# mLSTM branch: a block's exponentials issued one step ahead of its scores, in halves of shared E buffers

## The chip, the cores and the metric

The kernel runs on one core of a Trainium2 chip. A core has five engines that each work through a queue of their own: TensorE (PE in the profile, with its weight loads shown apart as PEld), VectorE (DVE), ScalarE (ACT), GpSimd (POOL) and SyncE (SP), which here only issues DMAs. They run side by side and wait for one another through semaphores. The metric is the device time of one execution in microseconds (us); the time of a kernel is the median over several executions.

## The reference

One layer of a hybrid encoder block, 512 tokens by 1024 channels in float32. An RMS norm is followed by one wide projection; three token mixers take their parts of it: a bidirectional mLSTM, a neighbourhood attention on an 8 by 64 grid, and a cross-attention into 256 memory tokens. Their outputs are gated, merged and projected, and a convolutional GLU feed-forward layer follows.

The change lies in the mLSTM. Per head and direction, with log gates `log_i`, `log_f` and their running sum `a`, it computes

```
D = a[..., :, None] - a[..., None, :] + log_i[..., None, :]
D = jnp.where(causal, D, -jnp.inf)
qk = jnp.einsum('bhcjd,bhcsd->bhcjs', q, k)
P = jnp.exp(D - m_j[..., None]) * qk
num = jnp.einsum('bhcjs,bhcsd->bhcjd', P, v) + inter_w[..., None] * (state of earlier chunks times q)
h = num / jnp.maximum(jnp.abs(den), jnp.exp(-m_j))[..., None]
```

where `den` is the same sum with the normaliser in place of `v`. There are four heads of width 128 and two directions whose results are added.

## The kernel before, in words

**The work as a whole.** TensorE does nearly everything that takes long. A float32 product is made of three matmuls on operands that were split into a high and a low part (`mm3`, lines 212 to 215). Weights come from HBM in 141 blocks of 512 KB and some smaller ones (line 159, issued by SyncE, three buffers); ScalarE copies the high part (L195) and VectorE subtracts to get the low part (L196). Both have to keep ahead of TensorE, and everything else that the two engines do is queued between these splits.

**The mLSTM inside it.** The generator `ml_all` gives the mLSTM in small steps, which the main program runs between projections through `step`. The kernel uses chunks of 128 tokens, so a head has four blocks, J = 0 to 3. The gates are prepared once (`ml_prep`, `spread`). Then, for each head:

- `load_head` loads two 128x512 tiles `R`, one for each direction, with the row part of the log weights spread over all partitions (L660). Four such buffers exist, so head h+2 uses those of head h, once their last reader is done. The cross-attention, which comes later, takes its split operands `X` from the same four buffers (tag "R", `prep` in `xa_all`, splits at L219 and L220).
- `mask` adds the causal mask to `R` (L666), `edges` makes the weights of the edge blocks (L673, L675), `keys` splits the keys and weighs the values (L681 to L704), and `states` computes the states at the block ends (L722 to L736, splits at L219 and L220).
- `weights_J` makes a block's weights: the score matmul on TensorE (L748), two exponentials on ScalarE, one for each direction (L752, 128x128 each), and on VectorE the product of the two (L753).
- `values_J` multiplies them with the values on TensorE (L761, and L763 for the edge state), takes the absolute denominator (L774 or L776), floors and inverts it (L778, L779), and scales and sums the outputs (L780 to L785, squares at L787).
- `normalise` takes the norm's power on GpSimd (L793), the scaling by it follows on ScalarE (L798), and `emit_y` transposes and splits the branch's result (L806, L808).

`weights_J` of block J+1 stands ahead of `values_J` of block J. The tile `E` (128 x 4 x 128, two buffers) is taken anew for each block, which uses the first half of it; the second half stays empty here, since the neighbourhood attention, which shares the tag, needs the full width later.

**What sets the order.** A scheduler orders the instructions of each engine when the kernel is built, from the program's order, the dependencies and the buffers that are free by its own account of time. On the chip each engine then works in that fixed order. `issue_after(st["act"])` only keeps the exponentials behind the last one of `spread`.

Of the kernel before, what the change touches and what calls it, by code (L numbers as in the profile page):

```python
# [11 lines left out]
F32 = mybir.dt.float32  # L12
F32R = mybir.dt.float32r
AF = mybir.ActivationFunctionType
# [3 lines left out]
P = 128  # L18
S = 512
# [91 lines left out]
def hybrid_block(ctx, tc, xg, xT, memT, wflat, vecs, gbias, nabias, outa, outb, outc):  # L111
    nc = tc.nc
    V, A, G, PE, SY = nc.vector, nc.scalar, nc.gpsimd, nc.tensor, nc.sync
# [5 lines left out]
    tp = ctx.enter_context(tc.tile_pool(name="tp", bufs=2))  # L119
# [6 lines left out]
    def nm(s):  # L126
        uid[0] += 1
        return f"{s}_{uid[0]}"
# [7 lines left out]
    def tiny(n):  # L136
        return tp.tile([P, 32], F32, tag="tiny", name=nm("y"), bufs=12)[:, :n]
# [4 lines left out]
    def atps():  # L142
        return atp.tile([P, 512], F32, tag="at", name=nm("at"))
# [4 lines left out]
    st = {"raw": 0, "split": 0}  # L148
# [262 lines left out]
    for k in range(KT):  # L411
# [12 lines left out]
        for f in range(4):  # L424
            fs = slice(f * P, (f + 1) * P)
            if k == 0 and f == 0:
                hs = (slice(0, S // 2), slice(S // 2, S))
# [118 lines left out]
    ml = {}  # L546
# [105 lines left out]
    def ml_all():  # L652
# [3 lines left out]
        def load_R(h):  # L656
            R = []
            for d in range(2):
                t = tp.tile([P, S], F32, tag="R", name=nm("R"), bufs=4)
                SY.dma_start(t, rd[d, h].partition_broadcast(P))  # L660
                R.append(t)
            return R
# [5 lines left out]
        def edges(h, R, ee):  # L668

            mh, eq = ml["mh"], ee[:, :2 * P].rearrange("p (i c) -> p i c", i=2)  # L670
            for i in range(2):
                J, d = 3 * i, 1 - i
                A.activation(eq[:, i, :], R[d][:, J * P:(J + 1) * P], AF.Exp, bias=mh[:, J - 1 + 2 * d, d, h:h + 1])  # L673
            qe = qT[:, h * S:(h + 1) * S].rearrange("p (j c) -> p j c", j=4)[:, 0:4:3, :]
            V.tensor_tensor(eq, eq, qe, op=ALU.mult)  # L675
# [35 lines left out]
        def states(h, k, w, C, q, eq, R):  # L711

            flush()
            dec = ml["dec"]
            (ke, kh, kl), (ew, wh, wl) = k, w
            pc = [atps() for _ in range(2)]
            po = (0, 130, 0, 131)
            at = lambda J, d: pc[J // 2][:, po[J] + 129 * d:po[J] + 129 * d + 129]
            for J in range(NT):
                if J in (0, 3):  # L720
                    e = J // 3
                    PE.matmul(at(J, e), ke[:, e * P:(e + 1) * P], ew[e], start=True, stop=True)  # L722
                else:
                    o, js = po[J], slice((J - 1) * P, J * P)
                    mm3(pc[J // 2][:, o:o + 258], kh[:, js], kl[:, js], wh[J - 1], wl[J - 1], True, True)
            tj = [tp.tile([P, 2 * M], F32, tag="nab", name=nm("C")) for _ in range(2)]
            pair = lambda j, d: tj[j][:, 129 * d:129 * d + 129]
            one = [t[:, 258:387] for t in tj]
            C.extend([[pair(0, 0), pair(1, 0), one[0]], [one[1], pair(0, 1), pair(1, 1)]])
            for d in range(2):  # L730
                last = None
                for i in range(3) if d == 0 else range(2, -1, -1):
                    if last is None:
                        A.activation(C[d][i], at(i + d, d), AF.Copy)
                    else:
                        V.scalar_tensor_tensor(C[d][i], C[d][last], dec[:, d, i + d - 1, h:h + 1], at(i + d, d),  # L736
                                               op0=ALU.mult, op1=ALU.add)
                    last = i
            for j in range(2):
                split_act(wh[j], wl[j], tj[j][:, :258])  # L740

        def weights_J(h, J, R):

            bi = ml["bi"]
            js, hs = slice(J * P, (J + 1) * P), slice(h * S + J * P, h * S + (J + 1) * P)
            ps = atps()
            kq = ps[:, 384:512]
            PE.matmul(kq, kT[:, hs], qT[:, hs], start=True, stop=True)  # L748
            E = tp.tile([P, 4, P], F32, tag="E", name=nm("E"))[:, 0:2, :]
            for d in range(2):  # L750
                with tc.issue_after(st["act"]):
                    A.activation(E[:, d, :], R[d][:, js], AF.Exp, bias=bi[:, d, J, h:h + 1])  # L752
            V.tensor_tensor(E, E, kq.unsqueeze(1).to_broadcast([P, 2, P]), op=ALU.mult)  # L753
            return E, ps

        def values_J(h, J, E, ps, k, w, C, q, eq, R, H, ss):
            js = slice(J * P, (J + 1) * P)
            pv = ps[:, :260].rearrange("p (d c) -> p d c", d=2)
            for d in range(2):
                inter = (J, d) in ((0, 1), (NT - 1, 0))  # L760
                PE.matmul(pv[:, d, 0:129], E[:, d, :], va[:, J, h, 0:129], start=True, stop=not inter)  # L761
                if inter:
                    PE.matmul(pv[:, d, 0:129], eq[:, J // (NT - 1), :], C[d][J - 1 + d], start=False, stop=True)  # L763
            den = tiny(2)
            both = J in (1, 2)
            if both:
                pi = mmps()[:, :258]
                qs = slice((J - 1) * P, J * P)
                mm3(pi, q[0][:, qs], q[1][:, qs], w[1][J - 1], w[2][J - 1], True, True)
                pi = pi.rearrange("p (d c) -> p d c", d=2)  # L770
                sc = ml["sc"][:, J, :, h]
                V.tensor_tensor(den, pi[:, :, 128], sc, op=ALU.mult)
                V.tensor_tensor(den, den, pv[:, :, 128], op=ALU.add)
                A.activation(den, den, AF.Abs)  # L774
            else:
                A.activation(den, pv[:, :, 128], AF.Abs)  # L776
            emv = em[:, J, :].rearrange("p (a b) -> p a b", b=4)
            V.tensor_tensor(den, den, emv[:, 0:9:8, h], op=ALU.max)  # L778
            V.reciprocal(den, den)  # L779
            A.activation(H[:, js], pv[:, 0, 0:128], AF.Copy, scale=den[:, 0:1])  # L780
            V.scalar_tensor_tensor(H[:, js], pv[:, 1, 0:128], den[:, 1:2], H[:, js], op0=ALU.mult, op1=ALU.add)
            if both:
                V.tensor_tensor(den, den, sc, op=ALU.mult)
                for d in range(2):
                    V.scalar_tensor_tensor(H[:, js], pi[:, d, 0:128], den[:, d:d + 1], H[:, js], op0=ALU.mult, op1=ALU.add)  # L785
            sq = scr(128)
            A.activation(sq, H[:, js], AF.Square, accum_out=ss[:, J:J + 1])  # L787

        def normalise(H, ss):
            v = tiny(4)  # L790
            V.tensor_scalar(v, ss, 1.0 / 128.0, EPS, op0=ALU.mult, op1=ALU.add)
            rs = tiny(4)
            G.tensor_tensor(rs, v, nhalf[:, :4], op=ALU.pow)  # L793

            def scale():
                for J in range(NT):
                    js = slice(J * P, (J + 1) * P)
                    A.activation(H[:, js], H[:, js], AF.Copy, scale=rs[:, J:J + 1])  # L798

            late.append(scale)  # L800
# [13 lines left out]
        prev = None  # L814
        E = None
        def load_head(h):
            return load_R(h), tp.tile([P, S], F32, tag="H", name=nm("ee"), bufs=4)
# [4 lines left out]
        for h in range(4):  # L822
            if prev:
                values_J(h - 1, 3, *E, *own, *prev)
                normalise(*prev)
            states(h, *st_h)
            own = st_h
            R = own[-1]
            ee, nxt = nxt[1], load_head(h + 1) if h < 3 else None
            yield  # L830
            H = tp.tile([P, S], F32, tag="H", name=nm("H"), bufs=4)
            ss = tiny(4)
            if h == 0:
                edges(0, R, ee)
                for d in range(2):
                    mask(R, d)
            E = weights_J(h, 0, R)
            yield
            for J in range(1, NT):
                E2 = weights_J(h, J, R)  # L840
                if J == 3 and h < 3:
                    st_h = keys(h + 1, *nxt)
                values_J(h, J - 1, *E, *own, H, ss)
                E = E2
                if J == 1 and prev:
                    emit_y(h - 1, prev[0])
                if h < 3:
                    late.append((lambda g=h + 1, n=nxt: edges(g, *n), lambda n=nxt: mask(n[0], 0),
                                 lambda n=nxt: mask(n[0], 1))[J - 1])
                yield  # L850
            prev = (H, ss)
# [223 lines left out]
    yml = []  # L1075
    so = []
    gens.append(ml_all())

    xq = unit()
# [427 lines left out]
```

## Time and profile before

| | us |
|---|---|
| time before, median of 3 runs (875.71 to 876.38) | 876.06 |
| the profiled execution's own time | 875.70 |
| its span, first to last instruction | 873.9 |
| first and last exponential of the mLSTM (L752) | 126.1 and 221.7 |
| first and last value matmul (L761) | 135.2 and 231.4 |

The difference of 1.8 between the profiled time and its span lies around the span. The profile gives a page (busy time of each engine, 40 slices of the span, DMA queues, the chain that ended last, the costliest groups) and answers on the trace: who waited for whom, busy time by stage, and a timeline in which a row holds the start in us, the length in us, the engine, the line of the code, the operation, out<-in by tile names, the number of instructions that the row holds, and in brackets the idle time of the engine before it with what ended it. Lengths of neighbouring instructions overlap by some 0.1 us on ScalarE and VectorE, so the cost of an instruction in a full queue is the distance from its start to the next one's start.

### The profile page before, as it was taken

The numbers are of one execution on the slowest core, as the hardware profiler recorded it, in microseconds if no ns is written. First come the engines' busy times: TensorE is split into PE (matmuls) and PEld (weight loads), VectorE is DVE, ScalarE is ACT, GpSimd is POOL, SyncE is SP. The second block draws the span as 40 slices with busy tenths as digits, with TensorE's granted clock in tenths as the row PEclk, the third lists the DMA queues.
The fourth block names the chain that finished last, engine by engine and source line by source line (L and its number), as shares of the span: only waits on it lengthen the run. The fifth ranks groups of instructions, "written<-read, shape, count | busy, mean of one in ns | idle before, by whom it ended". The sixth has DMA issues, their size and how long they took to land.

```text
span 873.9 us, 12229 instructions
## 1 busy us (share of the span) xinstructions
PE 868.1 (99%) x4303; PEld 736.2 (84%) x4303; DVE 594.2 (68%) x1240; ACT 472.7 (54%) x996; POOL 125.2 (14%) x201
## 2 busy tenths in 40 slices
PE   9999999999999999999999999999999999999997
PEld 7898888888888888888888888888888888888887
DVE  7794789886677758897676658776633466666534
ACT  7563567765456658888544455444422344444532
POOL 0101100000163370600000002111100011111010
PEclk9999999999999999999999999999999999999999
DMA  8224633422242353533223432222233222222412
GB/s 281 99 77 148 210 123 125 166 82 90 95 132 81 111 161 108 158 120 122 98 97 109 145 108 97 97 97 96 76 100 104 107 97 97 97 97 90 142 34 97
DMA packets 39421, 99.81 MB, mean 114 GB/s; under 512 B 5688, under 2 KB 13880, under 8 KB 39360
## 3 DMA queue, kind: packets, MB, share of 16 engines
q1 hardware_dynamic: 31568, 92.32, 30.7%
q0 software_dynamic: 7360, 6.32, 3.2%
q8 instruction: 34, 0.56, 0.3%
q10 hardware_dynamic: 432, 0.39, 0.1%
q14 instruction: 27, 0.22, 0.1%
HBM read 94.80 MB, written 4.21 MB: 113 GB/s over the span
## 4 chain that ended last, share of the span: by engine, by line
PE 94%; DVE 3%; ACT 1%; issue 1%; DMA 1%; POOL 0%; POOLq 0%; SPq 0%
PE mm L214 28%; PE mm L213 28%; PE mm L215 28%; PE at L214 2%; PE at L215 2%; PE at L213 2%; PE at L938 1%; PE at L919 1%; PE at L761 1%; DMA R<-rd 1%; DVE wl L196 0%; PE at L900 0%; PE at L901 0%; PE at L1026 0%; PE at L243 0%
## 5 line engine op out<-in xcount | busy, mean ns | idle before, releaser
L213 PE MATMUL mm<-u,wh 128*128 128x512 f32 (+1 forms) x1072 | 414.6, 387 | 0.0
L215 PE MATMUL mm<-u,wl 128*128 128x512 f32 (+1 forms) x1072 | 411.9, 384 | 0.0
L214 PE MATMUL mm<-u,wh 128*128 128x512 f32 (+1 forms) x1072 | 411.6, 384 | 0.0
L195 ACT ACTIVATE wh<-wr 128x512 fp32r<-128x512 f32 (+2 forms) x298 | 183.9, 621 | 213.5 <-PE mm L214 168.2
L196 DVE TENSOR_TENSOR wl<-wr,wh 128x512 fp32r<-128x512 f32 (+3 forms) x300 | 203.9, 681 | 89.5 <-ACT wh L195 86.7
L215 PEld LDWEIGHTS mm<-u,wl 128*128 128x128 f32 x1072 | 201.4, 188 | 40.0
L213 PEld LDWEIGHTS mm<-u,wh 128*128 128x128 f32 x1072 | 201.6, 188 | 38.6 <-ACT wh L195 0.2
L214 PEld LDWEIGHTS mm<-u,wh 128*128 128x128 f32 x1072 | 201.6, 188 | 38.4
L1371 POOL TENSOR_TENSOR s<-s,rb 128x512 f32<-128x512 f32 x22 | 38.1, 1732 | 403.4 <-DVE s L1370 239.0
L542 POOL DMA_DIRECT2D u<-nav_d x128 | 62.5, 533 | 66.2 <-PE at L938 23.0
L219 ACT ACTIVATE u<-s 128x512 fp32r<-128x512 f32 x26 | 16.4, 632 | 57.7 <-DVE s L1374 56.2
L1374 DVE TENSOR_TENSOR s<-mm,s 128x512 f32<-128x512 f32 x22 | 15.2, 690 | 23.8 <-POOL s L1371 23.8
L462 ACT ACTIVATE s<-pad,vec 128x512 f32<-128x512 f32 x30 | 24.4, 813 | 9.4 <-DVE pad L460 9.4
L220 DVE SCALAR_TENSOR_TENSOR u<-s,u 128x512 fp32r<-128x512 f32 x26 | 19.1, 733 | 14.1 <-ACT u L219 14.0
L463 DVE SCALAR_TENSOR_TENSOR s<-pad,vec,s 128x512 f32<-128x512 f32 x30 | 22.5, 750 | 5.4 <-ACT s L462 5.2
L1370 DVE SCALAR_TENSOR_TENSOR s<-s,s 128x512 f32<-128x512 f32 x22 | 15.2, 692 | 13.4 <-ACT s L1369 13.3
L464 DVE SCALAR_TENSOR_TENSOR s<-pad,vec,s 128x512 f32<-128x512 f32 x30 | 22.5, 750 | 0.9
L1369 ACT ACTIVATE s<-s 128x512 f32<-128x512 f32 x22 | 13.9, 632 | 14.9 <-DVE s L1368 14.9
L460 DVE TENSOR_TENSOR pad<-mm,rb 128x512 f32<-128x512 f32 x22 | 15.1, 690 | 6.4 <-PE mm L215 6.2
L213 PE MATMUL mm<-wh,u 128*128 128x512 f32 x48 | 18.8, 392 | 0.0
L215 PE MATMUL mm<-wh,u 128*128 128x512 f32 x48 | 18.7, 390 | 0.0
L214 PE MATMUL mm<-wl,u 128*128 128x512 f32 x48 | 18.7, 390 | 0.0
(341 smaller groups left out, 1043.6 us busy)
## 6 DMA issues: line engine op xcount, KB each, us to landing
wr<-wflat SPq DMA_DIRECT2D x141, 512.0 KB, 3.2
nab<-nabias SPq DMA_DIRECT2D x16, 256.0 KB, 2.6
u<-nav_d POOLq DMA_DIRECT2D x128, 32.0 KB, 2.6
s<-xT SPq DMA_DIRECT2D x15, 256.0 KB, 3.7
wr<-wflat SPq DMA_DIRECT2D x14, 192.0 KB, 2.3
nav_d<-nv POOLq DMA_DIRECT2D x8, 256.0 KB, 3.0
R<-rd SPq DMA_DIRECT2D x8, 256.0 KB, 4.6
wr<-wflat SPq DMA_DIRECT2D x2, 544.0 KB, 3.1
```

Source lines behind the costliest of these rows:

```text
L195: A.activation(h[:, u:v], src, AF.Copy)
L196: V.tensor_tensor(l[:, u:v], src, h[:, u:v].bitcast(F32), op=ALU.subtract)
L213: PE.matmul(ps, lh, rh, start=start, stop=False)
L214: PE.matmul(ps, lh, rl, start=False, stop=False)
L215: st["mm"] = PE.matmul(ps, ll, rh, start=False, stop=stop).ins
L219: A.activation(h, src, AF.Copy, scale=scale)
L220: V.scalar_tensor_tensor(l, src, scale, h.bitcast(F32), op0=ALU.mult, op1=ALU.subtract)
L462: A.activation(t1, pad[:, 0:512], AF.Identity, scale=vcol(w, i), bias=vcol(b, i))
L463: V.scalar_tensor_tensor(t1, pad[:, 1:513], vcol(w, n + i), t1, op0=ALU.mult, op1=ALU.add)
L464: V.scalar_tensor_tensor(t1, pad[:, 2:514], vcol(w, 2 * n + i), t1, op0=ALU.mult, op1=ALU.add)
L542: G.dma_start(vw[r * 32:(r + 1) * 32, i * 256:(i + 1) * 256], nav_v[hf, r, CW[b]:CW[b] + 32, hp * 256:(hp + 1) * 256])
L1371: G.tensor_tensor(c, c, rb2, op=ALU.mult)
```

## The change

The two exponentials leave `weights_J` and become a function of their own, `expos(h, J, R)`. It takes a new `E` buffer for J = 0 and 2 only, and gives block J the half `J % 2` of it, so two buffers hold four blocks. It is called one step earlier than before: for J = 0 behind `states` of the head (for head 0 behind its masks), and for J = 1 to 3 behind `weights_J` of the block before.

```
--- before.py
+++ after.py
-        def weights_J(h, J, R):
+        Eb = []
+
+        def expos(h, J, R):
+
+            if J % 2 == 0:
+                Eb[:] = [tp.tile([P, 4, P], F32, tag="E", name=nm("E"))]
+            E = Eb[0][:, J % 2 * 2:J % 2 * 2 + 2, :]
+            for d in range(2):
+                with tc.issue_after(st["act"]):
+                    A.activation(E[:, d, :], R[d][:, J * P:(J + 1) * P], AF.Exp, bias=ml["bi"][:, d, J, h:h + 1])
+            return E
+
+        def weights_J(h, J, E):
...
-            E = tp.tile([P, 4, P], F32, tag="E", name=nm("E"))[:, 0:2, :]
-            for d in range(2):
-                with tc.issue_after(st["act"]):
-                    A.activation(E[:, d, :], R[d][:, js], AF.Exp, bias=bi[:, d, J, h:h + 1])
             V.tensor_tensor(E, E, kq.unsqueeze(1).to_broadcast([P, 2, P]), op=ALU.mult)
             return E, ps
...
             ee, nxt = nxt[1], load_head(h + 1) if h < 3 else None
+            if h > 0:
+                En = expos(h, 0, R)
             yield
...
                 for d in range(2):
                     mask(R, d)
-            E = weights_J(h, 0, R)
+                En = expos(0, 0, R)
+            E = weights_J(h, 0, En)
+            En = expos(h, 1, R)
             yield
             for J in range(1, NT):
-                E2 = weights_J(h, J, R)
+                E2 = weights_J(h, J, En)
+                if J < 3:
+                    En = expos(h, J + 1, R)
                 if J == 3 and h < 3:
                     st_h = keys(h + 1, *nxt)
                 values_J(h, J - 1, *E, *own, H, ss)
```

No instruction is added or removed. What moves is seen in the built programs. On TensorE and GpSimd the order stays, but for one matmul: in head 2 the third matmul of a group (L215) now stands ahead of the value matmuls of block 0 (L761) and not behind them. On SyncE the two `R` loads of head 2 stand two to three weight blocks earlier, those of head 3 three. On ScalarE and VectorE the order changes in each head. ScalarE's queue in head 0, from its first exponential on (J and d are block and direction; line numbers are those of before):

```
before                                  after
L752 J0 d0                              L752 J0 d0
L1089 tanh, L311                        L1089 tanh, L311
L752 J1 d0                              L752 J1 d0, J2 d0, J3 d0
L693, L703 x2, L734, L703               L693, L734, L703
L219, L195, L219                        L219, L195, L219
L752 J0 d1, J1 d1                       L752 J0 d1, J1 d1, J2 d1, J3 d1
L703                                    L703 x2
L195                                    L195
table load, L337 (Ln)                   table load, L337 (Ln)
table load, L1089 tanh, L338            table load, L1089 tanh, L338
L195 x2                                 L195, L703, L195
L752 J2 d0, L1089, L776, L752 J2 d1     L776, L1089
L780                                    L780
```

And the two queues ahead of head 2's first product of scores and exponentials:

```
ScalarE before                          ScalarE after
L219 state, L798 x4, L219 state         L798 x4, L219 state, L219 state
L195                                    L195, L703, L219 X (128x512)
L195                                    L195

VectorE before                          VectorE after
L220 state, L736, L220 state            L736, L220 state, L220 state
L196                                    L196, L704, L220 X (128x512)
L1121, L753 J0, L753 J1                 L1121, L753 J0, L753 J1
```

Ahead of that stretch, and ahead of the same one in heads 1 and 3, ScalarE has the exponentials of blocks 2 and 3 of the head where it had those of block 1. Ahead of head 3's first product the two queues also get the two 128x256 splits of `X`.

More of the change, by code (lines that the diff above doesn't have):

```diff
@@ L740, in states @@
                 split_act(wh[j], wl[j], tj[j][:, :258])
-        def weights_J(h, J, R):
-            bi = ml["bi"]
-            js, hs = slice(J * P, (J + 1) * P), slice(h * S + J * P, h * S + (J + 1) * P)
+        Eb = []
[8 more added lines that the diff above has]
+        def weights_J(h, J, E):
+            hs = slice(h * S + J * P, h * S + (J + 1) * P)
             ps = atps()
```

## The prediction

> **What bounds the kernel now.** I read the page first, then the waits of TensorE and of its weight loads, then the busy time by stage, and last the timelines of ScalarE, VectorE and TensorE around the few places where TensorE waits inside the mLSTM. The page:
>
> ```profile
> PE 868.1 (99%) x4303; PEld 736.2 (84%) x4303; DVE 594.2 (68%) x1240; ACT 472.7 (54%) x996; POOL 125.2 (14%) x201
> ...
> PEclk9999999999999999999999999999999999999999
> ```
>
> TensorE is never without work for long and holds its full clock. What it waited for because of the weights `E`, from the list of waits (engine and line, what released it, us in total, times, longest):
>
> ```profile
> PE at L761 <- DVE E L753: 0.4, 1, 0.4
> ...
> PEld at L761 <- DVE E L753: 1.1, 3, 0.6
> ...
> ACT E L752 <- PE at L761: 3.7, 5, 1.5
> ```
>
> The first two rows are all the waits of TensorE that the exponentials can have a part in: at most 1.5 us, and the two overlap, since a weight load and its matmul wait for the same product. So the change has at most 0.17% to win. What it can lose is not bounded in this way, because ScalarE and VectorE work in a fixed order and the first one is asked to do things earlier than they are needed. The stage with the largest wait, from the busy time by stage (length, then busy us of PE, PEld, DVE, ACT, POOL, then granted clock):
>
> ```profile
> 135.00:145.00 10.00, 9.59 (x60) 8.40 (x59) 9.59 (x29) 7.22 (x22) 0.83 (x1) 1.00 0.33 119
> ```
>
> VectorE is as full there as TensorE, and TensorE's missing 0.41 is the wait of the first list.
>
> **Head 0: a pair of table loads moves back.** ScalarE in head 0 is busy without a gap from the first exponential to the tanh of the output gate:
>
> ```profile
> 129.99 0.68 ACT L752 ACTIVATE E<-R,bi 128x128 f32<-128x128 f32 x2
> 130.58 0.39 ACT L703 ACTIVATE u<-u,wt 128x129 fp32r<-128x129 f32 x1
> 130.87 0.62 ACT L195 ACTIVATE wh<-wr 128x512 fp32r<-128x512 f32 x1
> 131.51 1.28 ACT L337 ACT_TABLE_LOAD   x1
> 132.80 0.38 ACT L337 ACTIVATE s<-at 128x256 f32<-128x256 f32 x1
> 133.20 1.28 ACT L1089 ACT_TABLE_LOAD   x1
> 134.50 0.63 ACT L1089 ACTIVATE s<-s 128x512 f32<-128x512 f32 x1
> ```
>
> Start to start, two exponentials cost 0.59 and one L703 0.29. In the new order the four exponentials of blocks 2 and 3 stand ahead of these table loads (4 x 0.295 = 1.18), and one L703 has gone behind them (0.29). So the tanh starts 0.89 later, at 135.39. VectorE's queue behind it:
>
> ```profile
> 133.46 0.61 DVE L704 SCALAR_TENSOR_TENSOR u<-u,wt,u 128x129 fp32r<-128x129 f32 x2
> 135.16 0.43 DVE L1098 TENSOR_SCALAR u<-s 128x512 f32<-128x512 f32 x1 [1.09 <-ACT s L1089]
> ...
> 140.06 0.35 DVE L781 SCALAR_TENSOR_TENSOR H<-at,y,H 128x128 f32<-128x128 f32 x1 [0.25 <-ACT H L780]
> ...
> 143.10 0.41 DVE L753 TENSOR_TENSOR E<-E,at 128x256 f32<-128x256 f32 x1
> ```
>
> VectorE idles for that tanh already, and then works nearly without a gap up to the product at 143.10, so the product moves with the tanh. Of the stretch between them the new order takes out the idle 0.25 ahead of L781 (the floor and the reciprocal, L778 and L779, stand further ahead) and puts in one L704 (0.27, half of the distance in its row, moved back from 133.46). With some hundredths of rounding the product of block 2 starts 0.83 later, at 143.93. Its exponentials, which are early now, were not what it waited for. TensorE's rows there:
>
> ```profile
> 142.55 0.60 PE L681 MATMUL at<-ident,u 128*128 128x128 f32 x4
> 143.56 0.71 PE L761 MATMUL at<-u,E 128*128 128x129 f32 x4 [0.41 <-DVE E L753]
> ```
>
> The value matmul starts 0.46 after the product does, so it goes from 143.56 to 144.39, and the idle time from 0.41 to 1.24: **+0.83**.
>
> **Head 2: the splits of X come ahead of the product.** The exponentials read `R`, and when they are done early, head 2's `R` buffers come free some 13 us earlier, so the scheduler moves the first split of the cross-attention, which takes these buffers, ahead. It was here, in the middle of head 2:
>
> ```profile
> 194.24 0.62 ACT L219 ACTIVATE X<-u 128x512 fp32r<-128x512 f32 x1
> ...
> 194.89 0.69 DVE L220 SCALAR_TENSOR_TENSOR X<-u,X 128x512 fp32r<-128x512 f32 x1
> ```
>
> It now stands here, ScalarE and then VectorE:
>
> ```profile
> 183.16 1.28 ACT L798 ACTIVATE H<-H,y 128x128 f32<-128x128 f32 x4 [0.74 <-POOL y L793]
> 184.35 0.41 ACT L219 ACTIVATE u<-C 128x258 fp32r<-128x258 f32 x1
> 184.66 0.62 ACT L195 ACTIVATE wh<-wr 128x512 fp32r<-128x512 f32 x1
> ```
>
> ```profile
> 184.78 0.43 DVE L220 SCALAR_TENSOR_TENSOR u<-C,u 128x258 fp32r<-128x258 f32 x1 [1.64 <-ACT u L219]
> 185.30 0.69 DVE L196 TENSOR_TENSOR wl<-wr,wh 128x512 fp32r<-128x512 f32 x1
> 185.91 0.68 DVE L1121 TENSOR_TENSOR u<-mm,rb_x 128x512 f32<-128x512 f32 x1
> 186.51 0.74 DVE L753 TENSOR_TENSOR E<-E,at 128x256 f32<-128x256 f32 x2
> ```
>
> ScalarE reaches L798 at the same time, since that waits for GpSimd's power; the two more exponentials of this head fall into the wait of 0.74 and the place of two L703. Both state splits now follow it: 184.35 and 184.66, L195 at 184.97 (0.53), L703 at 185.50 (0.29), the split of X from 185.79 to 186.41. VectorE: the state splits at 184.78 and 185.12, L196 when ScalarE's copy is done (184.97 + 0.62 = 185.59) at 185.62, to 186.22, L704 (0.27) to 186.49, X (0.61) to 187.10, L1121 (0.60) to 187.70. The product starts 1.19 later than at 186.51, and there is no slack:
>
> ```profile
> 186.72 0.40 PE L214 MATMUL mm<-u,wh 128*128 128x512 f32 x1
> 186.98 0.71 PE L761 MATMUL at<-u,E 128*128 128x129 f32 x4
> ```
>
> TensorE starts 0.47 after the product, at 188.17. The one matmul that the new order puts ahead of it fills no more than the 0.26 between these rows, up to 187.24. So **+0.93**.
>
> **Head 3, the loads, and the sum.** Two 128x256 splits of X and two exponentials come ahead of L798 here:
>
> ```profile
> 210.52 1.28 ACT L798 ACTIVATE H<-H,y 128x128 f32<-128x128 f32 x4 [0.70 <-POOL y L793]
> ...
> 213.72 0.69 DVE L1126 SCALAR_TENSOR_TENSOR u<-mm,rb_x 128x512 f32<-128x512 f32 x1 [0.36 <-PE mm L215]
> ```
>
> On ScalarE's own path to L798 (exponentials, one X split of some 0.31, squares) it is 0.6 later, after what idle time that path had; ahead of the product VectorE had 0.36 to spare, and another 0.1 in the split ahead: +0.11. In head 1 the extra pair falls into the like waits, so nothing. The third row of the wait list is ScalarE waiting for the buffers of `E`; with four halves the exponentials of a head's block 0 wait for the value matmuls of block 1 of the head before, behind them in the queue stand denominators and weight splits of the next block but one, and ScalarE has waited there all along: 0. On SyncE the `R` loads of head 2 now wait for exponentials that end at about 131.3, and the weight block behind them was issued only at
>
> ```profile
> 133.57 0.33 SPq L159 DMA_DIRECT2D wr<-wflat  x1
> ```
>
> so nothing is held up: 0. The larger buffers of `E` cost nothing, as they were already of this size: 0. The sum is 0.83 + 0.93 + 0.11 = 1.87 on a profiled execution of 875.70 (span 873.9, 1.8 around it), so 877.6; that execution lay 0.36 under the median, so the median goes from 876.06 to **877.9**, +0.21%. The bounds: of the first term nothing is left if VectorE catches up, and it is at most 1.18 if the L703 does not help; the second runs from 0 to 1.19 + 0.27 (one more L704); the third from 0 to 0.31 + 0.6. Below nothing the listed waits give 1.5. That is 874.6 to 879.2; I take the replayed values, as each step is an instruction of known length in a full queue.
>
> The Trainium skill, in "Perfetto Trace Analysis", section "Identifying the Most-Contended Engine", says that TensorE's headroom is to be judged by the busy share of its weight loads and not by that of the matmuls. By it the 84% of the page's PEld would leave room in which such stalls could vanish, and the time would stay at 876.06. The trace does not agree: in the stage quoted above the idle 0.41 of TensorE stands beside weight loads at 8.40 of 10.
>
> **The rivals.** *Not slower: the early exponentials pay.* If VectorE's products were late because of their exponentials, the waits of 1.5 would go, in the overlap some 0.8, and the time would be 875.2 (-0.1%). It is decided at 143.10: the product must start no later than there. For it speaks that exponentials did stand close ahead of products; against it that each product's row follows VectorE's own work without idle time. Chance 0.08. *Only one stall grows.* If ScalarE has the slack ahead of the second state split that L798's wait suggests, or TensorE's own delay of 0.83 covers part of head 2's, the sum is 0.8 to 1.0 and the time 877.0. What counts is whether X is done by VectorE before 186; I find 187.1. Chance 0.20. *Stalls are absorbed* because TensorE has headroom: 876.1; against it the row above. Chance 0.05. *More stalls.* The extra pairs in heads 1 and 3 are not covered by the waits for GpSimd: head 1's weight splits, then head 3's product are later by another 0.6 each, and the time is 879.0. Against it stand the 0.74 and 0.70 in the L798 rows. Chance 0.15.
>
> **How the numbers follow.** The forecast has the other 0.52, with its own range 877.4 to 878.5. For 8 in 10, I leave out what ends under 876.5 (the first and third rival, 0.13) and the top of the last: 876.5 to 879.1. A change of 0.2%, 1.75 us, is about what a measurement of this kernel tells from none, so the line lies at 877.81, close under the forecast. Slower by more: three quarters of the forecast's own chance (0.39; a delay that I have not found can only add), all of "more stalls" (0.15) and a tenth of the one-stall case (0.02), 0.56. Faster by more would need more than the waits hold: 0.03, out of the first rival. The rest, 0.41, lies within.
>
> **What would show it.** Right: TensorE's wait for L753 in head 0 grows from 0.4 to about 1.2, and a new one of about 0.9 stands in head 2 behind an X split on VectorE; the table loads start near 132.4; TensorE's idle time in the mLSTM grows by 1.9 and nothing changes after about 240. Wrong: those waits shrink, or L753 waits for exponentials, or a stall stands at weight splits or elsewhere.

## The result and the profile after

The changed kernel takes 877.80 us (median of 15 runs, 877.34 to 878.45), the kernel before 875.80 us on the same occasion (15 runs, 875.28 to 876.41). The ratio is 1.0023 with a 95% interval of 1.0015 to 1.0031: slower by 0.23%, 2.0 us. The profiled execution has a span of 875.8 us, 1.9 more than before.

The page of the changed kernel, its busy time and the granted clock:

```profile
PE 868.1 (99%) x4303; PEld 736.3 (84%) x4303; DVE 594.8 (68%) x1240; ACT 471.5 (54%) x996; POOL 125.1 (14%) x201
...
PEclk9999999999999999999999999999999999999999
```

TensorE does the same work at the same clock, so the loss is idle time. The lists of waits (who waited for whom, us in total, times, longest):

```profile
PE at L768 <- DVE E L760: 2.3, 2, 1.3
...
PEld at L768 <- DVE E L760: 3.3, 3, 1.5
...
ACT E L751 <- PE at L768: 0.3, 1, 0.3
```

TensorE waits for the product of scores and exponentials twice, 2.3 us in all, where it was once and 0.4. ScalarE's waits for the buffers of `E`, 3.7 us before, are down to 0.3: this is what four halves do for ScalarE. It won no time: TensorE's one wait of before, for VectorE's product, did not get shorter. The stage of head 0 by busy time (length, then PE, PEld, DVE, ACT, POOL and the clock):

```profile
135.00:145.00 10.00, 8.74 (x53) 7.55 (x52) 9.21 (x27) 6.89 (x20) 0.84 (x1) 1.00 0.24 91
```

TensorE's 9.59 of 10 has become 8.74. ScalarE's queue in head 0 (start, length, instruction):

```profile
126.94 0.97 ACT L751 ACTIVATE E<-R,bi 128x128 f32<-128x128 f32 x3
...
129.74 1.27 ACT L751 ACTIVATE E<-R,bi 128x128 f32<-128x128 f32 x4
...
131.50 0.62 ACT L195 ACTIVATE wh<-wr 128x512 fp32r<-128x512 f32 x1
132.13 1.28 ACT L337 ACT_TABLE_LOAD   x1
...
133.83 1.28 ACT L1102 ACT_TABLE_LOAD   x1
135.12 0.63 ACT L1102 ACTIVATE s<-s 128x512 f32<-128x512 f32 x1
```

and VectorE's, up to the product of block 2:

```profile
135.78 0.43 DVE L1111 TENSOR_SCALAR u<-s 128x512 f32<-128x512 f32 x1 [2.23 <-ACT s L1102]
...
143.68 0.41 DVE L760 TENSOR_TENSOR E<-E,at 128x256 f32<-128x256 f32 x1
```

Behind head 0's first exponential, seven now stand ahead of the table loads (three and four) where there were three (one and two). VectorE idles 2.23 for the tanh where it idled 1.09, and the product follows at the end of a full queue.

**Distances in place of positions.** Two profiled executions do not run at the same place, even where their queues are the same: the first value matmul of head 0 starts at 135.17 before and at 135.74 in the run "the early call alone" below, whose queues are those of before; over all runs it lies between 134.86 and 135.74. Positions can't be compared to a tenth, distances can. TensorE's rows of before: the value matmuls of head 0's blocks 0 and 1, of head 1's last block, of head 3's block 0 and last block, and the last transposes:

```profile
135.17 0.61 PE L761 MATMUL at<-u,E 128*128 128x129 f32 x4
...
141.52 0.61 PE L761 MATMUL at<-u,E 128*128 128x129 f32 x4
...
178.31 0.38 PE L761 MATMUL at<-u,E 128*128 128x129 f32 x2
...
214.87 0.64 PE L761 MATMUL at<-u,E 128*128 128x129 f32 x4
...
230.82 0.38 PE L761 MATMUL at<-u,E 128*128 128x129 f32 x2
...
868.91 0.38 PE L1285 MATMUL mm<-ident,u 128*128 128x128 f32 x2
```

The same of the changed kernel, with the two that wait:

```profile
134.90 0.61 PE L768 MATMUL at<-u,E 128*128 128x129 f32 x4
...
141.24 0.61 PE L768 MATMUL at<-u,E 128*128 128x129 f32 x4
...
144.14 0.71 PE L768 MATMUL at<-u,E 128*128 128x129 f32 x4 [1.26 <-DVE E L760]
...
178.90 0.38 PE L768 MATMUL at<-u,E 128*128 128x129 f32 x2
...
188.98 0.71 PE L768 MATMUL at<-u,E 128*128 128x129 f32 x4 [1.04 <-DVE E L760]
...
216.68 0.71 PE L768 MATMUL at<-u,E 128*128 128x129 f32 x4
...
232.73 0.38 PE L768 MATMUL at<-u,E 128*128 128x129 f32 x2
...
870.82 0.38 PE L1298 MATMUL mm<-ident,u 128*128 128x128 f32 x2
```

| stretch, start to start | before | after | difference |
|---|---|---|---|
| head 0, block 1 to block 2 | 2.04 | 2.90 | +0.86 |
| from there to head 1's last block | 34.75 | 34.76 | 0 |
| from there through head 2 to head 3's block 0 | 36.56 | 37.78 | +1.22 |
| head 3, block 0 to its last | 15.95 | 16.05 | +0.10 |
| from there to the last transposes | 638.09 | 638.09 | 0 |
| all, from head 0's block 0 | 733.74 | 735.92 | +2.18 |

Distances are taken between starts, so an instruction that TensorE reaches late counts whether or not the list of waits has it. The loss sits in the mLSTM alone, at the two waits and a tenth in head 3, and the 638 us behind it give nothing back and add nothing.

In head 2 the queues of the changed kernel ahead of the product, ScalarE and then VectorE:

```profile
179.20 0.63 ACT L195 ACTIVATE wh<-wr 128x512 fp32r<-128x512 f32 x1 [0.29 <-PE mm L215]
...
183.99 1.28 ACT L805 ACTIVATE H<-H,y 128x128 f32<-128x128 f32 x4 [0.87 <-POOL y L800]
185.18 0.71 ACT L219 ACTIVATE u<-C 128x258 fp32r<-128x258 f32 x2
...
186.61 0.61 ACT L219 ACTIVATE X<-u 128x512 fp32r<-128x512 f32 x1
```

```profile
187.05 0.35 DVE L704 SCALAR_TENSOR_TENSOR u<-u,wt,u 128x129 fp32r<-128x129 f32 x1
187.31 0.69 DVE L220 SCALAR_TENSOR_TENSOR X<-u,X 128x512 fp32r<-128x512 f32 x1
187.91 0.69 DVE L1134 TENSOR_TENSOR u<-mm,rb_x 128x512 f32<-128x512 f32 x1
188.51 0.75 DVE L760 TENSOR_TENSOR E<-E,at 128x256 f32<-128x256 f32 x2
```

Both state splits, one L703/L704 and the split of X stand ahead of it. The first row is new: a copy of weights starts 0.29 us late, which it did not before. The last section comes back to it.

### The profile page after: what moved, and what is told of

It reads as the page before. It is cut to its first block, busy times and chain, and to the rows that moved or that the text cites. A ratio compares the mean times of both kernels' runs of the same rounds, so it can differ in the third digit from the quotient of the medians.

```text
span 875.8 us, 12228 instructions
## 1 busy us (share of the span) xinstructions
PE 868.1 (99%) x4303; PEld 736.3 (84%) x4303; DVE 594.8 (68%) x1240; ACT 471.5 (54%) x996; POOL 125.1 (14%) x201
## 4 chain that ended last, share of the span: by engine, by line
PE 97%; DVE 1%; ACT 1%; issue 0%; POOL 0%; POOLq 0%
PE mm L213 29%; PE mm L215 28%; PE mm L214 28%; PE at L214 2%; PE at L213 2%; PE at L215 2%; PE at L951 1%; PE at L932 1%; PE at L768 1%; PE at L913 0%; PE at L914 0%; PE at L1039 0%; PE at L243 0%; PE mm L422 0%; PE at L759 0%
## 5 line engine op out<-in xcount | busy, mean ns | idle before, releaser
L215 PE MATMUL mm<-u,wl 128*128 128x512 f32 (+1 forms) x1072 | 411.8, 384 | 0.0
L214 PE MATMUL mm<-u,wh 128*128 128x512 f32 (+1 forms) x1072 | 411.6, 384 | 0.0
L196 DVE TENSOR_TENSOR wl<-wr,wh 128x512 fp32r<-128x512 f32 (+3 forms) x300 | 204.0, 682 | 87.7 <-ACT wh L195 85.2
L215 PEld LDWEIGHTS mm<-u,wl 128*128 128x128 f32 x1072 | 201.4, 188 | 40.2
L214 PEld LDWEIGHTS mm<-u,wh 128*128 128x128 f32 x1072 | 201.6, 188 | 38.5
L215 PE MATMUL mm<-wh,u 128*128 128x512 f32 x48 | 18.7, 390 | 0.0
L214 PE MATMUL mm<-wl,u 128*128 128x512 f32 x48 | 18.7, 390 | 0.0
```

The costliest lines, as they stand in the source:

```text
L196: V.tensor_tensor(l[:, u:v], src, h[:, u:v].bitcast(F32), op=ALU.subtract)
L214: PE.matmul(ps, lh, rl, start=False, stop=False)
L215: st["mm"] = PE.matmul(ps, ll, rh, start=False, stop=stop).ins
```

## The experiments

Theory A is that of the prediction: the products are late because of what stands ahead of them in the fixed queues of ScalarE and VectorE. Rival B is that the halves, the shared tile or the earlier loads make the products late by themselves. A further question is which part of the change moves the queues. "Distance" in the text below is the last row of the table above, as a difference to before; each run's comparison has its own runs of the kernel before beside it.

**The halves alone.** The exponentials are called again with their block's scores; the four halves stay.

```
-            if h > 0:
-                En = expos(h, 0, R)
             yield
...
-                En = expos(0, 0, R)
-            E = weights_J(h, 0, En)
-            En = expos(h, 1, R)
+            E = weights_J(h, 0, expos(h, 0, R))
...
-                E2 = weights_J(h, J, En)
-                if J < 3:
-                    En = expos(h, J + 1, R)
+                E2 = weights_J(h, J, expos(h, J, R))
```

> The changed kernel with the exponentials called where they were before, with their block's scores, and only the four halves of the two E buffers kept. Theory A (what moves the queues is the room for four blocks, not the place of the call; the delays come from what stands ahead of VectorE's products): TensorE's wait for the product in head 0 is 1.26 us, in head 2 1.04 us, as in the changed kernel, and the time 877.8 us. Rival (the call one step earlier is what moves the exponentials ahead of the table loads): the waits are those of before, 0.4 us in all, and the time is 875.8 to 876.1 us.

Measured: 877.75 us against 876.00, ratio 1.0022 (1.0013 to 1.0031), distance +2.33. TensorE's waits:

```profile
PE at L768 <- DVE E L760: 2.5, 2, 1.4
```

The waits and the time are those of the changed kernel; the order of the instructions on every engine is the same too. So the edit that gave the change its name moves nothing. With room for four blocks the scheduler takes the exponentials early by itself, and it is the room that the change gives it.

**The early call alone.** Whole buffers, and the call as early as two of them allow.

```
-            if J % 2 == 0:
-                Eb[:] = [tp.tile([P, 4, P], F32, tag="E", name=nm("E"))]
-            E = Eb[0][:, J % 2 * 2:J % 2 * 2 + 2, :]
+            E = tp.tile([P, 4, P], F32, tag="E", name=nm("E"))[:, 0:2, :]
...
-                if J < 3:
-                    En = expos(h, J + 1, R)
...
                 values_J(h, J - 1, *E, *own, H, ss)
+                if J < 3:
+                    En = expos(h, J + 1, R)
```

> The exponentials called as early as two whole E buffers allow (behind the values of the block before the last), each block with a buffer of its own as before. Theory A: without room for more blocks nothing moves, one wait of 0.4 us in head 0, 875.8 to 876.1 us. Rival (the earlier call does it): the wait in head 0 grows towards 1.2 us and the time to 876.9 us or more.

Measured: 876.08 us, ratio 1.0002 (0.9994 to 1.0011), distance -0.03, one wait:

```profile
PE at L766 <- DVE E L758: 0.3, 1, 0.3
```

This is the kernel before, on every engine's queue and in time. The rival falls in both runs.

**Head 0's exponentials behind the table loads.** They are put behind the exponential of `rstd_wide` (L338), which follows the loads.

```
-        A.activation(y, v, AF.Exp, scale=-0.5)
+        st["tb"] = A.activation(y, v, AF.Exp, scale=-0.5).ins
...
-                with tc.issue_after(st["act"]):
+                with tc.issue_after(st["tb"] if h == 0 and J > 1 else st["act"]):
                     A.activation(E[:, d, :], R[d][:, J * P:(J + 1) * P], AF.Exp, bias=ml["bi"][:, d, J, h:h + 1])
```

> The changed kernel, but in head 0 the four exponentials of blocks 2 and 3 are put behind the pair of table loads on ScalarE. Theory A: the tanh starts near 134.5 us again instead of 135.1, the product of block 2 some 0.6 to 0.8 us earlier, TensorE's wait in head 0 falls from 1.26 to 0.4 us, that in head 2 stays near 1.0, time 876.9 to 877.1 us. Rival B (the halves share a tile, or the R loads that come earlier disturb: the products are late whatever stands ahead of the tables): the wait in head 0 stays at 1.2 us and the time at 877.8 us.

Measured: 877.09 us against 876.00, ratio 1.0012 (1.0003 to 1.0020), distance +1.20. TensorE's rows, blocks 0 to 2 of head 0, head 1's last block and head 2's block 0:

```profile
135.55 0.61 PE L768 MATMUL at<-u,E 128*128 128x129 f32 x4
...
141.90 0.61 PE L768 MATMUL at<-u,E 128*128 128x129 f32 x4
...
144.11 0.71 PE L768 MATMUL at<-u,E 128*128 128x129 f32 x4 [0.57 <-DVE E L760]
...
178.85 0.38 PE L768 MATMUL at<-u,E 128*128 128x129 f32 x2
...
188.66 0.71 PE L768 MATMUL at<-u,E 128*128 128x129 f32 x4 [0.76 <-DVE E L760]
```

The tanh and a copy of weights on ScalarE:

```profile
135.03 0.63 ACT L1102 ACTIVATE s<-s 128x512 f32<-128x512 f32 x1
...
178.89 0.63 ACT L195 ACTIVATE wh<-wr 128x512 fp32r<-128x512 f32 x1
```

From block 1 to block 2 it is 2.21 us, so 0.69 of the 0.86 is gone, inside the 0.6 to 0.8 expected; a wait of 0.57 is left where 0.4 was expected. The tanh's position of 135.03 looks unmoved, but this execution ran 0.65 later: the tanh starts 0.52 ahead of head 0's first value matmul, against 0.22 behind it in the changed kernel (0.67 ahead before). Rival B falls for head 0. A second gain was not expected: the copy of weights at 178.89 is not late, and the stretch through head 2 is 37.49 in place of 37.78. The last section shows that this second gain is an accident of the edit.

**VectorE's split of X behind head 2's products.**

```
-            V.tensor_tensor(E, E, kq.unsqueeze(1).to_broadcast([P, 2, P]), op=ALU.mult)
+            p = V.tensor_tensor(E, E, kq.unsqueeze(1).to_broadcast([P, 2, P]), op=ALU.mult).ins
+            if (h, J) == (2, 1):
+                st["x"] = p
...
-        q, k = prep(0)
+        with tc.issue_after(st["x"]):
+            q, k = prep(0)
```

> The changed kernel, but VectorE's 128x512 split of X is kept behind head 2's products of blocks 0 and 1; ScalarE's part of it stays early. Theory A: the product starts 0.60 us earlier, TensorE's wait in head 2 falls from 1.04 to 0.4 to 0.7 us (the third matmul of a group stands behind the value matmuls again and no longer covers 0.2 of it), the wait in head 0 stays 1.26, time 877.2 us. Rival B (not VectorE's queue but the later state split on ScalarE or the shared tile holds the product): the wait stays near 1.0 and the time at 877.8 us.

Measured: 877.56 us against 876.00, ratio 1.0019 (1.0010 to 1.0027), distance +1.71. VectorE, then TensorE:

```profile
188.10 0.74 DVE L760 TENSOR_TENSOR E<-E,at 128x256 f32<-128x256 f32 x2
...
189.36 0.69 DVE L220 SCALAR_TENSOR_TENSOR X<-u,X 128x512 fp32r<-128x512 f32 x1
```

```profile
188.56 0.71 PE L770 MATMUL at<-u,E 128*128 128x129 f32 x4 [0.68 <-DVE E L760]
...
189.25 0.48 PE L215 MATMUL mm<-u,wl 128*128 128x512 f32 x1
```

The product starts 9.02 us after head 1's last value matmul (at 179.08) in place of 9.61: 0.59 for the 0.60 of the split, as expected, so Rival B falls in head 2 too. The stretch through head 2 is shorter by only 0.37, since the third matmul of the group, which ran ahead of the value matmul in the changed kernel, is behind it again and costs its 0.23 there. The wait was forecast rightly, the time 0.36 too low: the expectation took the 0.60 off the time without giving the 0.23 back.

**Both edits.**

```
+                with tc.issue_after(st["tb"] if h == 0 and J > 1 else st["act"]):
...
+        with tc.issue_after(st["x"]):
+            q, k = prep(0)
```

> Both edits in the changed kernel: head 0's exponentials of blocks 2 and 3 behind the pair of table loads, and VectorE's 128x512 split of X behind head 2's products. If the two delays are separate and add up (theory A): TensorE's waits are about 0.5 and 0.7 us, 1.2 in all against 2.3, and the time is 876.7 us. If one covers part of the other (rival C), the gain is no more than that of the first edit alone, and the time 877.1 us.

Measured: 876.46 us against 875.79, ratio 1.0008 (0.9999 to 1.0017), distance +0.67.

```profile
PE at L770 <- DVE E L760: 0.8, 2, 0.4
```

The distances of the two single edits are shorter than that of the changed kernel by 0.98 and 0.47, that of both by 1.51: the two delays add up, and neither covers the other. The waits are 0.41 and 0.40, where 0.5 and 0.7 were expected, since the copy of weights is not late here either; that is 0.29 of the 0.98 and of the 1.51. What is left is 0.55 through head 2 (37.11 against 36.56) and 0.1 in head 3. The 0.55 is near what the prediction's sum keeps without X (1.19 less 0.60, for the later state splits and the L703 and L704 that came ahead), but no run takes these out, so their part is argued and not shown.

**The `R` tiles held longer.** Nothing is told to the split of X; its buffers only come free later (`st["e2"]` is the last product made).

```
                 if J < 3:
                     En = expos(h, J + 1, R)
+                if (h, J) == (2, 1):
+                    for d in range(2):
+                        with tc.issue_after(st["e2"]):
+                            V.tensor_copy(tiny(1), R[d][:, 0:1])
```

> The changed kernel with two more reads of head 2's R tiles (one column each, on VectorE, behind the product of its block 1), so that these buffers do not come free before. Theory A (X came ahead because its buffers were free): the split of X stands behind the product on both engines without being told to, TensorE's wait in head 2 is 0.6 to 0.7 us in place of 1.04, and the time 877.4 to 877.6 us, as with the split held back by hand. Rival (the split moved for another reason than its buffers): it stays ahead of the product, and so does the wait of 1.0.

Measured: 877.56 us against 875.79, ratio 1.0022 (1.0013 to 1.0030), distance +1.83. ScalarE's and VectorE's rows:

```profile
188.89 0.63 ACT L219 ACTIVATE X<-u 128x512 fp32r<-128x512 f32 x1 [1.53 <-DVE y L857]
```

```profile
188.05 0.74 DVE L760 TENSOR_TENSOR E<-E,at 128x256 f32<-128x256 f32 x2
188.71 0.21 DVE L857 COPY y<-R 128x1 f32<-128x1 f32 x2
...
189.55 0.69 DVE L220 SCALAR_TENSOR_TENSOR X<-u,X 128x512 fp32r<-128x512 f32 x1
```

The split waits for the last reader of `R` and stands behind the product on both engines; TensorE's wait in head 2 is 0.67. So X came ahead because its buffers were free, as the prediction had it. The ratio alone does not show it, the gain of 0.35 in distance being 0.04% of the time; the rows do.

**Head 1's masks behind head 0's product of block 2**, in the changed kernel and in the one before (`p` is the product, in `weights_J`).

```
+            if (h, J) == (0, 2):
+                st["e"] = p
...
-            V.tensor_tensor(r4, r4, msk[d].unsqueeze(1).to_broadcast([P, 4, P]), op=ALU.add)
+            with tc.issue_after(st.get("e", st["act"])):
+                V.tensor_tensor(r4, r4, msk[d].unsqueeze(1).to_broadcast([P, 4, P]), op=ALU.add)
```

> The changed kernel with the two masks of head 1 (128x512 on VectorE, 0.60 us each) kept behind head 0's product of block 2; ScalarE's queue ahead of the table loads as in the changed kernel. Theory A (the product waits for nothing but the work ahead of it on VectorE): the product starts 1.2 us earlier, TensorE's wait in head 0 falls from 1.26 to 0.1 us or none, time 876.6 us. Rival B (the product waits for its operands, the exponentials or the scores): the wait stays at 1.2 us, time 877.8 us. What is not known is the price of later masks in head 1; if it is paid, a new wait stands between 150 and 170 us.

Measured: 876.56 us against 875.79, ratio 1.0010 (1.0001 to 1.0019), distance +0.98.

```profile
142.70 0.41 DVE L761 TENSOR_TENSOR E<-E,at 128x256 f32<-128x256 f32 x1
```

```profile
143.16 0.71 PE L771 MATMUL at<-u,E 128*128 128x129 f32 x4 [0.33 <-DVE E L761]
```

The product starts 1.50 after the value matmul of block 1 (at 141.20) where it was 2.44, so its operands had long been there. The gain is 0.94 and not 1.2, since VectorE then reached a weight split (L196) before ScalarE's copy was done. The later masks cost nothing; the stretch through head 2 is 37.50, without the 0.29 again. That makes up for the smaller gain, so the time agrees with the forecast by luck.

> The kernel before with the same edit of the masks. Theory A: the only wait of TensorE for a product, 0.41 us in head 0, is gone, the time is 875.4 to 875.7 us, which a measurement of this kernel can hardly tell from 876.0. Rival B: the wait stays. A price of the later masks in head 1 would show as a new wait between 150 and 170 us.

Measured: 875.39 us against 875.79, ratio 0.9996 (0.9986 to 1.0005), distance -0.47.

```profile
143.29 0.71 PE L764 MATMUL at<-u,E 128*128 128x129 f32 x4
```

The matmul waits for nothing. TensorE is busy 120.00 us of 120 between 120 and 240, the median is the lowest of all, and the interval still holds 1: the trace shows the gain, the medians can't.

All kernels side by side (TensorE's waits for the product; difference of the distance; difference of the median to before on the same occasion; us):

| kernel | waits | distance | median |
|---|---|---|---|
| changed | 2.3 | +2.18 | +2.00 |
| halves alone | 2.5 | +2.33 | +1.75 |
| early call alone | 0.3 | -0.03 | +0.08 |
| head 0 behind the tables | 1.3 | +1.20 | +1.09 |
| X behind the product | 1.8 | +1.71 | +1.56 |
| both | 0.8 | +0.67 | +0.67 |
| `R` held | 1.9 | +1.83 | +1.77 |
| masks late, changed | 1.1 | +0.98 | +0.77 |
| masks late, before | none | -0.47 | -0.40 |

## Why the prediction was right

The time, 877.8 against 877.9, and the sign were right, and the forecast's own mechanism is the one that the runs show. That the two times agree to 0.1 is in part luck: the forecast started from 876.06 for the kernel before, which took 875.80 beside the result, and its sum of 1.87 is below the difference of 2.00 between the medians and the 2.18 of TensorE's rows. Point by point:

- *What bounds the kernel.* Nothing speaks against it: no run won more than the listed waits hold (0.47 of distance when TensorE's only wait for a product was taken away), and the loss was not bounded by them.
- *Head 0, +0.83.* Measured +0.86. Against head 0's first value matmul the tanh is later by 0.89 (from 0.67 ahead to 0.22 behind), just the 4 x 0.295 less one L703 of the prediction; the product is later by 0.86, and TensorE's idle time went from 0.41 to 1.26, where 1.24 was forecast. Putting the exponentials back took away 0.69 of it, so this cause is shown. The early exponentials were not what the product had waited for, as the runs with the later masks show. A slip of the prediction lies within this term: its parts on VectorE (0.89, less 0.25, plus 0.27) add up to 0.91 and not to 0.83, and the 0.08 between was put down to rounding; the 0.86 lies between the two.
- *Head 2, +0.93.* Measured +1.22. In the runs whose weight copy is not late (head 0 behind the tables, masks late) it is 0.93 and 0.94, so the steps of the term were right and one was missing. Their sizes were a little off in both directions: in "head 0 behind the tables" the product is later by 1.14 (1.19 forecast), and the matmul that moved ahead covers 0.21 of it (0.26 forecast), two errors of 0.05 that cancel. The step that failed in the changed kernel is "ScalarE reaches L798 at the same time, since that waits for GpSimd's power": that power is taken of sums that ScalarE itself makes (L794 after the change), behind the copy of weights that starts 0.29 late. The last section shows what this goes with; it is not the work of the exponentials.
- *Head 3, +0.11.* Measured +0.10, in the stretch from block 0 to the last block. It lies at the product that the prediction named, though TensorE's own list has no wait there: it is the weight load of block 0's first value matmul that waits longer, 0.29 after the change where it was 0.20, and the four matmuls take 0.71 (216.68 above) where they took 0.64. The two weight loads, before and after:

```profile
214.79 0.52 PEld L761 LDWEIGHTS at<-u,E 128*128 128x128 f32 x4 [0.20 <-DVE E L753]
```

```profile
216.68 0.52 PEld L768 LDWEIGHTS at<-u,E 128*128 128x128 f32 x4 [0.29 <-DVE E L760]
```

  The parts that the prediction names (0.6 later, less 0.36 and 0.1) leave 0.14 and not 0.11, and no run tests this term by itself.
- *Nothing elsewhere.* Right: head 1 and all behind the mLSTM have the same distances to 0.01. The `R` loads that come earlier and the larger use of the buffers cost nothing that shows.
- *The sum.* 1.87 was forecast and the distance grew by 2.18; nearly all of the difference is the 0.29 of the copy. The profiled execution of the changed kernel was ahead by 0.27 at head 0, so its span shows 1.9. The widest range of the prediction counts its lower end from the median of before (876.06) and its upper end from the profiled execution (875.70); from the median the upper end is 879.6 and not 879.2.
- *The rivals.* "The early exponentials pay" fell: they came early, and no wait went. "Only one stall grows" fell: two did. "More stalls" was not met in the way it was described, though a third, smaller delay came in head 2. "Stalls are absorbed", the rival that the prediction set beside the Trainium skill ("Perfetto Trace Analysis", section "Identifying the Most-Contended Engine", which names MFU, a share of the peak arithmetic rate, beside the busy share of the weight loads), fell: with weight loads at 84% of the span both before and after, each us of TensorE's waits came back as about one us of time, over nine kernels (in the changed one 1.9 more of waits and 2.18 more of distance).
- *What it did not see.* The prediction spoke of the change as one; the runs show that the earlier call does nothing and the halves do all of it. This did not alter the number, because the order was read from the built queues and not from the diff.

A row of the trace that the prediction leaned on is the table load, 1.28 us, with the tanh 1.29 after the start of the second. The Trainium skill, "ScalarE: Activation LUTs", section "What ACT_TABLE_LOAD costs", gives 1283 ns for the load, which agrees, and some 2.66 us for every switch to a different set, a drain of some 1380 ns included. No such drain shows here: the weight copy ahead starts at 131.50 and lasts 0.62, the first load starts at 132.13, and the measured rows decide.

## What to carry to other kernels

Where a scheduler orders the instructions, as here, more room for a result can be an order to produce it earlier, whether the program asks for that or not; and whatever is produced early stands ahead of something else in a fixed queue, and can free its inputs' buffers for work that then comes ahead as well. Follow the readers of the moved instruction's inputs, not only those of its result: the split of another branch that took the freed buffers held the product for 0.60, and cost 0.37 of the 2.18 us, since the matmul that moved ahead covers 0.23. In a kernel whose TensorE is 99% busy, list its few waits first: here they held all that any run won, and the loss from the delays on the other engines was larger than all of them.

## What the runs showed that was not expected

- Profiled executions with the same queues reach the same place up to 0.6 us apart (135.17 and 135.74 at head 0's first value matmul), though in all ten kernels TensorE's distances over the stretches of 34.75 and 638.09 us agree to 0.02. Start-to-start distances in one execution resolved effects of 0.1 us, for which the medians of 11 runs, with intervals of some 0.09% to either side (0.8 us), are too coarse.
- TensorE's waits in the list understate a delay where the matmul ahead is counted with its full length: in head 2 the list has 1.04 and the stretch grew by 1.22. The matmul ahead is counted with 0.40 there, and the next one in a full queue starts some 0.23 after it.
- The late copy of weights is found in the four kernels of ten that idle at least 1.1 us in head 0, as if that delay were its cause. The traces show something else. The copy waits for a semaphore of TensorE; in the built programs of all ten kernels that is the end of the same matmul, an L214. In the traces this semaphore is raised 0.08 us before the copy starts in the six other kernels and 0.36 before in these four, so the copy starts late though what it waits for is done. (The profile names the L215 behind it, which ends in between; in the six the copy starts before that L215 ends.) What differs is the copy's place in ScalarE's stream. Counted in the traces, semaphore waits included, it is ScalarE's 320th instruction in the four kernels and the 319th or 316th in the six. Two later copies that wait for TensorE behave alike in all ten kernels: the semaphore is raised 0.36 to 0.37 before where the copy is the 832nd instruction (four kernels, near 437 us) or the 1216th (three, near 800 us), and 0.08 before where it is the 825th, 833rd, 1223rd or 1224th. The kernel with `R` held has the 320th and the 832nd late, the changed one the 320th alone, the one before the 1216th alone. Only the 320th costs TensorE time. The three places lie 512 and 384 apart; what is special about them is not shown.
- So 0.29 of the loss of 2.18 is an accident of place, and the rest, 1.89, is what the forecast of 1.87 was about. The same holds for the second gain of "head 0 behind the tables", "both" and "masks late": their edits leave one semaphore wait fewer ahead of the copy, which moves it from the 320th place to the 319th.
